# First layer: projections on input times norm weight, with the root applied to the products

## The chip, the cores and the metric

The kernel runs on 1 core of one Trainium2 chip. The metric is the time of one execution on the device in microseconds (us); the whole network is one launch.

## What is computed

Sixteen meta tokens and 1,024 input tokens, each of width 1,024, go through four layers: windowed attention, an mLSTM, an HGRN2 and windowed attention again. Each layer normalizes its input and adds its output to it. The change touches the first layer, an attention layer:

```python
def rmsnorm(x, g):
    xf = x.astype(jnp.float32)
    y = xf * lax.rsqrt(jnp.mean(xf * xf, axis=-1, keepdims=True) + EPS)
    return (y * g.astype(jnp.float32)).astype(x.dtype)

# u = rmsnorm(h, norm_gain[i])
q, k, v, z = _split(u @ w_in, (A_W, A_KVW, A_KVW, A_W))
q = rope(rmsnorm(q.reshape(bsz, lp, A_HEADS, A_HD), q_gain), pos)
k = rope(rmsnorm(k.reshape(bsz, lp, A_KV, A_HD), k_gain), pos)
o = sliding_window_attention(q, k, v, sinks, valid)
return (o * jax.nn.silu(z.astype(jnp.float32))).astype(u.dtype) @ w_out
```

The root `rsqrt(...)` is one number for each token. It is a factor of the whole row of u, and so of q, k, v and z before their own norms and gates.

## The kernel before

The state `x` lies in SBUF with the model width on the partitions: eight tiles of 128 x 1,040 tokens. The tokens go in three chunks of 400, 384 and 256 (`CHUNKS`; chunk 0 has the 16 meta tokens in front). Every matrix is split into a high and a low part of a reduced float format (`split`: ScalarE casts, VectorE subtracts), and each product is three matmuls: high by high, low input by high weight, high input by low weight (`proj`, L228). The split input is `uh` and `ul`, the split weight `wh` and `wl`. Weights come in two raw pieces of 128x512 from two rotating buffers (`wr`, `RAWS`), loaded by SyncE's queue.

TensorE's order is written out by hand as a list of steps with costs: `chain`, `weave` and `later` place a projection's follow-up steps at a delay (`D_K` for keys, `D_Q` for queries) behind its matmuls. The other engines run what the steps issue, in an order that a scheduler sets from priorities and readiness at build time. All engines' queues are in order.

In the head of the first layer, for each chunk, one key tile (two heads) and two query tiles are projected. Before that, `Norm` makes the normalized input: ScalarE squares each tile of x (L352), the squares are added (L356, on VectorE for chunk 0, on GpSimd for chunks 1 and 2), TensorE sums over the partitions with a matrix of ones (L364), ScalarE takes the root by a logarithm and an exponential (L338, L339), and for each of the eight tiles VectorE multiplies x by gain and root (L386) and the result is split into `uh` and `ul`.

A query or key product is then evacuated from PSUM by ScalarE twice, with its gain (L492) and squared (L493); four DMAs on SyncE make a rotated copy (L496); TensorE sums the squares (`stat_q`, L516, tiny products for queries; `stat`, L525, a full one for keys); VectorE applies the rotation (L530 to L534) and splits the result for the scores (`qs`, and the key's rows). Behind the head comes the body: score steps S (L621, L622, then VectorE, an exponential on ScalarE and a product on GpSimd, L635), transposes T (L647) and value products V (L666), woven with the value, query, key and gate projections and the output projections. A gate's evacuation (`gate_proj`) is a sigmoid in five steps and two products on VectorE (L411, L412). The buffers `Sm`, `Ph` and `Pl` of the scores have two copies each, `tmp` tiles (t) six, PSUM eight, and `yh`, a pair of the output projections, three.

Of the kernel before, what the change touches and what calls it, by code (L numbers as in the profile page):

```python
# [15 lines left out]
P = 128  # L16
D = 1024
# [94 lines left out]
def hybrid_kernel(ctx: ExitStack, tc: tile.TileContext, ins, out, layers=(0, 1, 2, 3)):  # L112
# [35 lines left out]
    def psj():  # L148
        return psum("pj", 3)
# [9 lines left out]
    ngain = cpool.tile([P, 4, KT], F32, name="ngain")  # L159
    eps = cpool.tile([P, 1], F32, name="eps")  # L160
    v.memset(eps, EPS)
    one = cpool.tile([P, 1], F32, name="one")
    v.memset(one, 1.0)
# [5 lines left out]

    def load_x(n):  # L170
        c0, cn = CHUNKS[n]
        for k in range(KT):
            sp.dma_start(x[:, k, c0 : c0 + cn], ins["xT"][k, :, c0 : c0 + cn])

    load_x(0)
    sp.dma_start(ngain, ins["ngain"])

# [32 lines left out]

    def proj(src, evac, chunks=CHUNKS):
        st = {}

        def pre():
            st["w"] = weights(src, "m")

        groups = []
        for n, (c0, cn) in enumerate(chunks):
            grp = []
            for part in range(4):  # L220
                def fn(n=n, c0=c0, cn=cn, part=part):
                    if part == 0:
                        st[n] = psj()
                    h, l = st["w"]
                    acc = st[n]
                    for k in (2 * part, 2 * part + 1):
                        for i, (a, b) in enumerate(((h, uh), (h, ul), (l, uh))):
                            pe.matmul(acc[:, :cn], a[:, k, :], b[:, k, c0 : c0 + cn],  # L228
                                      start=(k == 0 and i == 0), stop=(k == KT - 1 and i == 2))
# [111 lines left out]
    class Norm:  # L341
        def __init__(self, i, row=None):
            self.i, self.row, self.acc, self.ps = i, row, {}, {}

        def sq(self, m, n, c0, cn, size=KT):
            if m % size:
                q = tmp()[:, :cn]
            elif self.row is not None and n:
                q = self.row[:, c0 : c0 + cn]
            else:  # L350
                q = (vtile() if n == 2 else tmp())[:, :cn]
            s.activation(q, x[:, m, c0 : c0 + cn], AF.Square)  # L352
            if m % size == 0:
                self.acc[n] = q
            else:
                (v if self.row is None or n == 0 else g).tensor_tensor(self.acc[n], self.acc[n], q, op=ALU.add)  # L356

        def stat(self, n, part=0, parts=1):
            cn = CHUNKS[n][1]

            def fn():
                if part == 0:
                    self.ps[n] = psa()
                pe.matmul(self.ps[n][:, :cn], ones, self.acc[n], start=(part == 0), stop=(part == parts - 1))  # L364
                if part == parts - 1:
                    rstd_from(self.ps[n], self.acc[n], cn, D)

            return [4 * cn * MM, fn, None]

        def squares(self, n, part=0, parts=1):  # L370

            size = KT // parts

            def fn():
                for m in range(part * size, (part + 1) * size):
                    self.sq(m, n, *CHUNKS[n], size)

            return [0.0, fn, None]

# [15 lines left out]
        def units(self, n, t0, t1):  # L395
            return [(t0 + (t1 - t0) * k / KT, self.unit(n, k)) for k in range(KT)]

    def sigmoid_from(z, cn):
        a = tmp()
# [6 lines left out]

    def gate_proj(src, o, chunks=CHUNKS):
        def evac(acc, n, c0, cn):
            cs = slice(c0, c0 + cn)
            a = sigmoid_from(acc[:, :cn], cn)  # L410
            v.tensor_tensor(a[:, :cn], a[:, :cn], acc[:, :cn], op=ALU.mult)  # L411
            v.tensor_tensor(o()[:, cs], o()[:, cs], a[:, :cn], op=ALU.mult)  # L412

        return proj(src, evac, chunks)

    def layer_a(i, j, first, last, fin):
        win, wout = ins["a_win"][j], ins["a_wout"][j]
# [67 lines left out]

        def qk_proj(src, gcol, work, fsplit, ch, t=None):
            late = {}

            def evac(acc, n, c0, cn):
                dst, sq, rot = work(n, c0, cn)  # L490
                late[n] = dst, sq, rot
                s.activation(dst, acc[:, :cn], AF.Identity, scale=R["cons"][:, gcol : gcol + 1])  # L492
                s.activation(sq, acc[:, :cn], AF.Square)  # L493
                for q in range(4):
                    o = q ^ 1
                    sp.dma_start(rot[32 * q : 32 * q + 32], dst[32 * o : 32 * o + 32])  # L496

            def finish(n, c0, cn):
                def factors():
                    b0, bn = CHUNKS[n]  # L500
                    if R.get("cs", (None,))[0] != n:
                        R["cs"] = n, R["mix"].tile([P, 2, 400], F32, tag="cs", name=nm("cs"), bufs=1)
                        sp.dma_start(R["cs"][1][:, :, :bn], ins["rope"][:, :, b0 : b0 + bn].rearrange("a p t -> p a t"))
                    late[n] += (R["cs"][1][:, :, c0 - b0 : c0 - b0 + cn],)

                def stat_q():
# [10 lines left out]
                    z = slice(2 if last and n == 0 else 0, 2 * nb)  # L517
                    s.activation(rq[:, z], st[:, z], AF.Ln, bias=eps, scale=1.0 / 64)
                    s.activation(rq[:, z], rq[:, z], AF.Exp, scale=-0.5)
# [17 lines left out]
                if t is not None:  # L537
                    return [(D_Q[0], [0.0, factors, None]), (D_Q[1], [108 * len(CHUNK_BLOCKS[n]), stat_q, None]),
                            (D_Q[2], [0.0, rope, None]), (D_Q[3], turn)]
                return [(D_K[0], [4 * cn * MM, stat, None]), (D_K[1], [0.0, rope, None]), (D_K[2], turn)]  # L540

            return proj(src, evac, ch), [finish(n, *c) for n, c in enumerate(ch)]

# [20 lines left out]
        def v_proj(src, jj):  # L564
# [7 lines left out]
            def finish(n, c0, cn):  # L572
                def fn():
# [4 lines left out]
                    for k, b in enumerate(CHUNK_BLOCKS[n]):  # L578
# [6 lines left out]
                        src = pt[:nq, P * k : P * k + P].rearrange("p (a c) -> p a c", a=2)  # L585
                        s.copy(parts[:, 0:4:3], src)
                        v.tensor_tensor(parts[:, 1:3], src, parts[:, 0:4:3].bitcast(F32), op=ALU.subtract)

# [105 lines left out]

        zc = {t: gate_proj(win[12 + t], lambda t=t: R["o", t], chunks) for t in range(8)}
# [3 lines left out]
        kg1, kfin1 = qk_proj(win[1], 1, tmps, k_split(1), CHUNKS)  # L699
        vg0, vfin0 = v_proj(win[2], 0)  # L700
        vg1, vfin1 = v_proj(win[3], 1)
        qg = {t: qk_proj(win[4 + t], 0, tmps, q_split(t), chunks, t) for t in range(8)}

# [11 lines left out]
        for n in range(3):  # L715
            parts = [([], ev), tile_of([k0[0][n]], [k0[1][n]]), tile_of([qa[0][n]], [qa[1][n]])]
            if first and n == 0:
                (a, fa), (b, fb) = parts[1:]
                ta = sum(z[0] for z in a)
                parts[1:] = [(a[:2] + b[:2] + a[2:] + b[2:], [(d + ta, z) for d, z in fa + fb])]  # L720
            if first:
                parts += [tile_of([qb[0][n]], [qb[1][n]])]
            elif n == 2:
                parts += [tile_of(*qb)]
            grp, ev = chain(parts)
            head.append(grp)
# [597 lines left out]

    norm = Norm(layers[0], row())

    for k in range(PARTS):
        steps += [norm.squares(0, k, PARTS), norm.stat(0, k, PARTS)]
    steps += [norm.unit(0, k) for k in range(KT)]
    tail = None  # L1330
    for pos, i in enumerate(layers):
# [10 lines left out]
        if i % 3 == 0:  # L1342
            head, body, oa, ob = layer_a(i, i // 3, tail is None, i == 3, fin)
        elif i % 3 == 1:
# [17 lines left out]
        else:  # L1362
            h0, h1 = (sum(z[0] for z in head[k]) for k in range(2))
            seq = flat(head)
            for n, t, h in ((2, h0, h1), (1, 0.0, h0)):
                t0, t1, t2 = (t + z * h for z in FIRST[n - 1])
                later(seq, (t0, norm.squares(n)), (t1, norm.stat(n)), *norm.units(n, t2, t + h))
            head = [seq]
# [5 lines left out]

    ahead, k = 0.0, 0
    while steps[k][2] is None:
        k += 1
    steps[k][2]()
    steps[k][2] = None
    load_x(1)  # L1380
    sp.dma_start(ident, ins["ident"])
    k = 0
    for n, (cost, fn, pre) in enumerate(steps):
# [119 lines left out]
```

## Time and profile before

| | |
|---|---|
| median of 3 runs | 2615.19 us (2614.67 to 2615.76) |
| the profiled execution's own time | 2615.34 us |
| its span | 2613.6 us |
| busy: TensorE, VectorE, ScalarE, GpSimd | 98%, 75%, 65%, 10% |
| first product of the head | 14.08 us |
| first product behind the head | 79.39 us |
| first score step S | 84.66 us |

A row of the timeline gives the start, the length, engine, line, operation, output and inputs, and in brackets the idle time of the engine before it and what ended that. A row of the groups gives a line's instructions: busy us, mean ns of one, and idle time before them. A row of the table by stretch gives the length and each engine's busy time. The busy time of TensorE counts matmuls that overlap and run at half speed, so the pace of products is read from their starts.

### The profile page before, as it was taken

The numbers are of one execution on the slowest core, as the hardware profiler recorded it, in microseconds if no ns is written. First come the engines' busy times: TensorE is split into PE (matmuls) and PEld (weight loads), VectorE is DVE, ScalarE is ACT, GpSimd is POOL, SyncE is SP. The second block draws the span as 40 slices with busy tenths as digits, with TensorE's granted clock in tenths as the row PEclk, the third lists the DMA queues.
The fourth block names the chain that finished last, engine by engine and source line by source line (L and its number), as shares of the span: only waits on it lengthen the run. The fifth ranks groups of instructions, "written<-read, shape, count | busy, mean of one in ns | idle before, by whom it ended". The sixth has DMA issues, their size and how long they took to land.

```text
span 2613.6 us, 54261 instructions
## 1 busy us (share of the span) xinstructions
PE 2565.6 (98%) x20422; PEld 2485.5 (95%) x20422; DVE 1952.1 (75%) x5248; ACT 1689.4 (65%) x4422; POOL 249.1 (10%) x502
## 2 busy tenths in 40 slices
PE   7999999999999999999999999999999999999999
PEld 6999999999999999999999999999999999999999
DVE  6797798785647474646465688988888978887996
ACT  6776767576555555554555757878675857767772
POOL 2221221000000000000000000101000000321330
PEclk8999999999999999999999999999999999999999
DMA  4212111021111111111111111111111113112112
GB/s 130 68 51 85 54 44 48 22 66 58 41 58 41 58 41 51 44 53 41 57 41 50 57 32 37 34 34 34 38 38 31 37 51 92 56 47 84 56 40 79
DMA packets 82582, 135.92 MB, mean 52 GB/s; under 512 B 12032, under 2 KB 35712, under 8 KB 82320
## 3 DMA queue, kind: packets, MB, share of 16 engines
q1 hardware_dynamic: 82320, 132.45, 16.3%
q8 instruction: 161, 2.64, 0.4%
q14 instruction: 101, 0.83, 0.1%
HBM read 117.56 MB, written 4.26 MB: 47 GB/s over the span
## 4 chain that ended last, share of the span: by engine, by line
PE 80%; DVE 9%; ACT 6%; DMA 2%; issue 2%; SPq 1%; POOL 0%; DVEq 0%; ACTq 0%; POOLq 0%
PE pj L228 39%; PE pj L322 16%; PE pj L277 10%; PE po L666 2%; PE pt L647 2%; PE po L909 1%; PE pa L923 1%; PE po L911 1%; PE pm L621 1%; ACT Sm L632 1%; PE pm L622 1%; DVE Sm L629 1%; PE pj L273 1%; PE pm L1161 1%; DMA cs<-in_rope 1%
## 5 line engine op out<-in xcount | busy, mean ns | idle before, releaser
L228 PE MATMUL pj<-uh,wh 128*128 128x256 f32 (+2 forms) x2688 | 915.2, 340 | 9.3 <-ACT uh L194 9.2
L228 PE MATMUL pj<-ul,wh 128*128 128x256 f32 (+2 forms) x2688 | 867.7, 323 | 2.1 <-DVE ul L195 1.9
L228 PE MATMUL pj<-uh,wl 128*128 128x256 f32 (+2 forms) x2688 | 864.6, 322 | 0.0
L228 PEld LDWEIGHTS pj<-uh,wh 128*128 128x128 f32 x2688 | 510.0, 190 | 26.0 <-ACT uh L194 12.5
L228 PEld LDWEIGHTS pj<-ul,wh 128*128 128x128 f32 x2688 | 510.1, 190 | 10.5 <-DVE ul L195 5.4
L228 PEld LDWEIGHTS pj<-uh,wl 128*128 128x128 f32 x2688 | 509.7, 190 | 0.0
L195 DVE TENSOR_TENSOR wl<-wr,wh 128x512 fp32r<-128x512 f32 (+1 forms) x338 | 233.6, 701 | 50.1 <-ACT wh L194 47.1
L194 ACT CAST wh<-wr 128x512 fp32r<-128x512 f32 (+1 forms) x338 | 202.9, 613 | 102.1 <-PE pj L322 32.7
L322 PE MATMUL pj<-yh,wh 128*128 128x384 f32 (+2 forms) x768 | 253.2, 330 | 8.2 <-DVE x L325 6.2
L325 DVE TENSOR_TENSOR x<-x,pj 128x384 f32<-128x384 f32 (+2 forms) x480 | 234.6, 507 | 35.0 <-PE pj L322 33.7
L322 PE MATMUL pj<-yh,wl 128*128 128x384 f32 (+2 forms) x768 | 245.5, 320 | 0.0
L322 PE MATMUL pj<-yl,wh 128*128 128x384 f32 (+2 forms) x768 | 245.5, 320 | 0.0
L277 PE MATMUL pj<-wh,uh 128*128 128x256 f32 (+1 forms) x768 | 232.2, 302 | 0.0
L277 PE MATMUL pj<-wl,uh 128*128 128x256 f32 (+1 forms) x768 | 216.5, 282 | 0.0
L277 PE MATMUL pj<-wh,ul 128*128 128x256 f32 (+1 forms) x768 | 216.2, 282 | 0.0
L635 POOL TENSOR_TENSOR Sm<-Sm,s 128x512 f32<-128x512 f32 (+2 forms) x136 | 142.2, 1046 | 450.6 <-DVE s L634 435.8
L632 ACT ACTIVATE Sm<-Sm,s 128x257 f32<-128x257 f32 (+2 forms) x272 | 130.8, 482 | 78.9 <-DVE s L629 74.7
L404 ACT ACTIVATE t<-t 128x384 f32<-128x384 f32 (+2 forms) x240 | 117.9, 491 | 82.9 <-DVE t L403 80.8
L403 DVE SCALAR_TENSOR_TENSOR t<-pj,t 128x384 f32<-128x384 f32 (+2 forms) x192 | 98.7, 514 | 80.1 <-ACT t L402 78.4
L322 PEld LDWEIGHTS pj<-yh,wh 128*128 128x128 f32 x768 | 144.5, 188 | 11.9 <-DVE x L325 7.3
L194 ACT CAST yh<-r 128x384 fp32r<-128x384 f32 (+2 forms) x120 | 57.1, 478 | 152.0 <-PE pj L322 139.9
L277 PEld LDWEIGHTS pj<-wh,uh 128*128 128x128 f32 x768 | 144.6, 188 | 2.2
(255 smaller groups left out, 5434.0 us busy)
## 6 DMA issues: line engine op xcount, KB each, us to landing
wr<-in_b_win SPq DMA_DIRECT2D x124, 256.0 KB, 2.9
wr<-in_a_win SPq DMA_DIRECT2D x80, 256.0 KB, 2.9
wr<-in_c_win SPq DMA_DIRECT2D x64, 256.0 KB, 2.7
wr<-in_a_wout SPq DMA_DIRECT2D x32, 256.0 KB, 2.8
wr<-in_b_wout SPq DMA_DIRECT2D x32, 256.0 KB, 2.8
t<-t SPq DMA_DIRECT2D x104, 48.0 KB, 1.9
cs<-in_rope SPq DMA_DIRECT2D x11, 400.0 KB, 3.4
cs<-in_rope SPq DMA_DIRECT2D x11, 384.0 KB, 3.4
```

Of the source, the lines that this page charges most:

```text
L194: s.copy(h, src)
L195: v.tensor_tensor(l, src, h.bitcast(F32), op=ALU.subtract)
L228: pe.matmul(acc[:, :cn], a[:, k, :], b[:, k, c0 : c0 + cn], start=(k == 0 and i == 0), stop=(k == KT - 1 and i == 2))
L277: pe.matmul(acc[:cn, :nc], a[:, k, c0 : c0 + cn], m[:, kk, :], start=(k == 0 and j == 0), stop=(k == KT - 1 and j == 2))
L322: pe.matmul(acc[:, :cn], a[:, k, mc], b, start=(k == 0 and i == 0), stop=(k == 1 and i == 2))
L325: v.tensor_tensor(x[:, m, c0 : c0 + cn], x[:, m, c0 : c0 + cn], acc[:, :cn], op=ALU.add)
L403: v.scalar_tensor_tensor(a[:, :cn], z, 0.0, a[:, :cn], op0=ALU.min, op1=ALU.subtract)
L404: s.activation(a[:, :cn], a[:, :cn], AF.Exp)
L632: s.activation(Sm[:nq, u, : nk + 1], Sm[:nq, u, : nk + 1], AF.Exp, scale=-1.0, bias=st[:nq, u : u + 1], accum_out=den[:nq, u : u + 1])
L635: g.tensor_tensor(Sm[:nq, :, :nk], Sm[:nq, :, :nk], den[:nq].rearrange("p (u c) -> p u c", c=1).to_broadcast([nq, 2, nk]), op=ALU.mult)
L647: pe.transpose(pt[:kn, ki, u, :nq], Sm[:nq, u, ko : ko + kn], ident[:nq, :nq])
L666: pe.matmul(po[:, :, q0 - g0 : q0 - g0 + nq], V[pair // 2, kb][:kn, P * hh : P * hh + P], w[part][:kn, ki, :, :nq], start=(ki == 0 and par ...
```

## The change

`Norm` serves the later layers alone. For the first layer a class `Scale` takes its place. It splits x times the gain, without the root (`unit`), so the products need nothing but x and the weights. Squares of x are made and added on GpSimd for chunks 0 and 2, and on ScalarE with adds on VectorE for chunk 1; they are written to the three `yh` buffers. `sums` makes the root later, as a row over the tokens and as columns for blocks of tokens, and stores the row in memory; `fetch` reads it back into all partitions. The root then comes behind the products: the key's evacuation and each gate's multiply by it on VectorE, the values' split takes it as a scale, and the query statistic adds a term with EPS in place of it, since the query's own norm removes it.

The head's order becomes query, query, key; the key's evacuation in the head is put off (`held`, `D_EVAC`), the chains behind it get longer delays, and query 1 writes into the scores' buffers `Ph`, `Pl` and `Sm` (`idle`). The loads go weights first, half of x, weights, the other half.

```diff
-PARTS = 4
-FIRST = (0.2, 0.8, 0.85), (0.2, 0.75, 0.8)
+FIRST = (0.3, 0.2, 0.9), (0.0, 1.1, 1.9)
+D_K0, D_K1 = (5000.0, 7000.0, 9000.0), (5000.0, 7000.0, 9000.0)
+D_Q0 = 5500.0, 8000.0, 7000.0, 9000.0
+D_EVAC = 3000.0
+SUMS = 1.22, 1.95, 2.95
...
+    class Scale:
...
+            def fn():
+                gain = ngain[:, self.i, k : k + 1]
+                s.activation(uh[:, k, cs], x[:, k, cs], AF.Identity, scale=gain)
+                v.scalar_tensor_tensor(ul[:, k, cs], x[:, k, cs], gain, uh[:, k, cs].bitcast(F32),
+                                       op0=ALU.mult, op1=ALU.subtract)
...
+                for m in range(KT):
+                    q = tpool.tile([P, 400], F32, tag="yh", name=nm("sq"), bufs=YS)[:, :cn] if m else acc
+                    z = x[:, m, c0 : c0 + cn]
+                    if n == 1:
+                        s.activation(q, z, AF.Square)
+                    else:
+                        g.tensor_tensor(q, z, z, op=ALU.mult)
+                    if m:
+                        (v if n == 1 else g).tensor_tensor(acc, acc, q, op=ALU.add)
...
+                for k, b in enumerate(bs):
+                    q0 = blk(b)[0] - c0
+                    pe.matmul(pc[:, k : k + 1], acc[:, q0 : q0 + P], ones[:, 0:1], start=True, stop=True)
+                r, e = (z[:, bs[0] : bs[-1] + 1] for z in (self.rcol, self.ecol))
+                s.activation(e, pc[:, : len(bs)], AF.Identity, bias=self.eps2, scale=EPS / D)
+                s.activation(r, pc[:, : len(bs)], AF.Ln, bias=eps, scale=1.0 / D)
+                s.activation(r, r, AF.Exp, scale=-0.5)
+                pr = psa()
+                pe.matmul(pr[:, :cn], ones, acc, start=True, stop=True)
+                rstd_from(pr, acc, cn, D)
+                sp.dma_start(self.dram[c0 : c0 + cn], acc[0:1])
...
+        def fetch(self, dst, c0, cn):
+            sp.dma_start(dst[:, :cn], self.dram[c0 : c0 + cn].partition_broadcast(P))
...
         def evac(acc, n, c0, cn):
             cs = slice(c0, c0 + cn)
-            a = sigmoid_from(acc[:, :cn], cn)
-            v.tensor_tensor(a[:, :cn], a[:, :cn], acc[:, :cn], op=ALU.mult)
+            z = acc[:, :cn]
+            if scale is not None:
+                z = rs[n][:, :cn]
+                v.tensor_tensor(z, z, acc[:, :cn], op=ALU.mult)
+            a = sigmoid_from(z, cn)
+            v.tensor_tensor(a[:, :cn], a[:, :cn], z, op=ALU.mult)
...
+        def idle(n, c0, cn):
+            z = [R["mix"].tile([P, 2, 2, P], F32, tag=z, name=nm(z), bufs=2) for z in ("Ph", "Pl")]
+            z = [y.rearrange("p a u q -> p (a u q)") for y in z]
+            z.append(R["mix"].tile([P, 2, 257], F32, tag="Sm", name=nm("Sm"), bufs=2).rearrange("p u k -> p (u k)"))
...
+                if first and t is None:
+                    v.tensor_tensor(sq, sq if fetched else scale.row[:, c0 : c0 + cn], z, op=ALU.mult)
+                    z = sq
...
+                        v.scalar_tensor_tensor(rq.rearrange("p (k c) -> p k c", c=2),
+                                               st[:, z].rearrange("p (k c) -> p k c", c=2), 1.0 / 64, e,
+                                               op0=ALU.mult, op1=ALU.add)
```

At the program's start, TensorE before sums squares (`pa`) ahead of the first product (`pj`):

```order
L364 MATMUL pa_148<-t_143,ones 128x400
L364 MATMUL pa_148<-t_150,ones 128x400
L364 MATMUL pa_148<-t_156,ones 128x400
L364 MATMUL pa_148<-t_162,ones 128x400
L228 MATMUL pj_211<-uh,wh_96 128x400
```

and now begins with the products:

```order
L232 MATMUL pj_214<-uh,wh_90 128x400 [waits Activation_49]
L232 MATMUL pj_214<-ul,wh_90 128x400 [waits DVE_49]
L232 MATMUL pj_214<-uh,wl_91 128x400
L232 MATMUL pj_214<-uh,wh_90 128x400 [waits Activation_49]
L232 MATMUL pj_214<-ul,wh_90 128x400 [waits DVE_49]
```

The sums moved behind; the first products wait for ScalarE's and VectorE's split of x alone.

On ScalarE in the head, before, the squares of chunk 1 (`t` from x) end ahead of the first key's and query's evacuations (`pj`):

```order
L352 ACTIVATE t_241<-x 128x384
L352 ACTIVATE t_244<-x 128x384
L352 ACTIVATE t_247<-x 128x384
L352 ACTIVATE t_250<-x 128x384
L492 ACTIVATE r_271<-pj_211,cons_207 128x400
L493 ACTIVATE r_272<-pj_211 128x400
L492 ACTIVATE t_292<-pj_224,cons_207 128x400
L493 ACTIVATE t_293<-pj_224 128x400
```

and now, behind the last split of x, whose high part is `uh` (`sq`: squares of chunk 1 in the `yh` buffers; `pj_214` and `pj_227`: the two queries' products of chunk 0):

```order
L401 ACTIVATE uh<-x,ngain 128x256 [waits DMAHW7_49]
L419 ACTIVATE sq_245<-x 128x384 [waits Pool_49]
L419 ACTIVATE sq_248<-x 128x384 [waits Pool_49]
L419 ACTIVATE sq_251<-x 128x384 [waits Pool_49]
L419 ACTIVATE sq_254<-x 128x384 [waits DVE_49]
L576 ACTIVATE t_280<-pj_214,cons_188 128x400 [waits DMAHW1_49,DVE_49,PE_49]
L419 ACTIVATE sq_257<-x 128x384 [waits DVE_49]
L419 ACTIVATE sq_260<-x 128x384 [waits DVE_49]
L419 ACTIVATE sq_263<-x 128x384 [waits DVE_49]
L577 ACTIVATE t_281<-pj_214 128x400
L576 ACTIVATE Ph_305<-pj_227,cons_188 128x400 [waits PE_49]
L577 ACTIVATE Pl_306<-pj_227 128x400
```

The squares of chunk 1 stand behind all splits and now wait for GpSimd, and the queries' evacuations stand behind the squares.

What they wait for is the end of GpSimd's queue in the head, the last squares of chunk 2 and their adds, which now has 30 operations ahead of the first copy for the scores (`Sm`):

```order
L421 TENSOR_TENSOR sq_205<-x 128x256 [waits DMAHW5_49]
L423 TENSOR_TENSOR r_86<-r_86,sq_205 128x256 [waits Pool_49]
L421 TENSOR_TENSOR sq_208<-x 128x256 [waits DMAHW6_49]
L423 TENSOR_TENSOR r_86<-r_86,sq_208 128x256 [waits Pool_49]
L421 TENSOR_TENSOR sq_211<-x 128x256 [waits DMAHW7_49]
L423 TENSOR_TENSOR r_86<-r_86,sq_211 128x256 [waits Pool_49]
```

where there were the adds alone, with the squares on ScalarE:

```order
L356 TENSOR_TENSOR r_95<-r_95,t_439 128x256
L356 TENSOR_TENSOR r_95<-r_95,t_442 128x256
L356 TENSOR_TENSOR r_95<-r_95,t_445 128x256
L356 TENSOR_TENSOR r_95<-r_95,t_448 128x256
L635 TENSOR_TENSOR Sm_804<-Sm_804,s_806 16x2x16
```

GpSimd's queue grew from 14 adds (of chunks 1 and 2) to 16 squares and 14 adds (of chunks 0 and 2).

More of the change, by code (lines that the diff above doesn't have):

```diff
@@ L223, in fn @@
                         st[n] = psj()
+                    if part == 1 and early is not None:
+                        early(n, c0, cn)
                     h, l = st["w"]
@@ L693, in mixers @@
             return segs
-        zc = {t: gate_proj(win[12 + t], lambda t=t: R["o", t], chunks) for t in range(8)}
+        zc = {t: gate_proj(win[12 + t], lambda t=t: R["o", t], chunks, scale) for t in range(8)}
         oc = {t: proj_out(wout[t - 1], wout[t], lambda k, t=t: R["o", t - 1 + k], chunks,
@@ L698, in layer_a @@
         kg0, kfin0 = qk_proj(win[0], 1, work_rows(3), k_split(0), CHUNKS)
-        kg1, kfin1 = qk_proj(win[1], 1, tmps, k_split(1), CHUNKS)
+        kg1, kfin1 = qk_proj(win[1], 1, tmps, k_split(1), CHUNKS, fetched=first)
         vg0, vfin0 = v_proj(win[2], 0)
         vg1, vfin1 = v_proj(win[3], 1)
-        qg = {t: qk_proj(win[4 + t], 0, tmps, q_split(t), chunks, t) for t in range(8)}
+        qg = {t: qk_proj(win[4 + t], 0, idle if first and t == 1 else tmps, q_split(t), chunks, t) for t in range(8)}
         def q_pair(p):
@@ L1323, in ahead_of_end @@
         steps[k:k] = first
[L1325 to L1329, printed above, removed]
+    norm = Scale(layers[0])
+    steps += [norm.unit(0, k) for k in range(KT)] + [norm.squares(0)]
     tail = None
@@ L1373, in hybrid_kernel @@
     steps += seq
[L1375 to L1379, printed above, removed]
+    pres = [z for z in steps if z[2] is not None]
+    for z, k0, k1 in ((pres[0], 0, 4), (pres[1], 4, 8)):
+        z[2]()
+        z[2] = None
+        load_x(0, k0, k1)
+    pres[2][2]()
+    pres[2][2] = None
     load_x(1)
     sp.dma_start(ident, ins["ident"])
-    k = 0
+    ahead, k = 0.0, 0
     for n, (cost, fn, pre) in enumerate(steps):
```

158 lines of the change are left out of this document (102 added, 56 removed).

## The prediction

> **What bounds the kernel now.** I read the page's totals, then busy time by stretch, then the timeline of the first 85 us, then the waits of TensorE.
>
> ```profile
> span 2613.6 us, 54261 instructions
> PE 2565.6 (98%) x20422; PEld 2485.5 (95%) x20422; DVE 1952.1 (75%) x5248; ACT 1689.4 (65%) x4422; POOL 249.1 (10%) x502
> ```
>
> TensorE is busy 98% of the span, so the end moves only by what TensorE waits or runs slowly. The timed execution took 2615.34 us, 1.7 us more than its span, and lies 0.15 us from the median of the runs, 2615.19; I carry the sum on 2615.34. The change touches the first layer alone, so I look for lost time there: length, then busy us and count of PE, PEld, DVE, ACT and POOL, then the granted clock, the DMA share and GB/s.
>
> ```profile
> 0.00:10.00 10.00, 4.28 (x6) 1.91 (x7) 2.73 (x8) 6.30 (x11) 0.52 (x5) 1.00 0.80 260
> 10.00:20.00 10.00, 6.89 (x18) 5.19 (x17) 8.29 (x16) 6.56 (x14) 0.17 (x1) 0.71 0.73 257
> 40.00:60.00 20.00, 16.32 (x75) 15.02 (x75) 13.92 (x27) 13.32 (x32) 5.80 (x7) 0.83 0.18 50
> 60.00:80.00 20.00, 17.20 (x84) 14.98 (x84) 13.23 (x30) 12.53 (x32) 0.00 (x0) 0.66 0.14 36
> 160.00:320.00 160.00, 159.58 (x1093) 155.66 (x1092) 130.22 (x333) 113.21 (x317) 34.91 (x54) 1.00 0.20 60
> 320.00:420.00 100.00, 96.22 (x685) 91.93 (x684) 90.71 (x258) 73.06 (x217) 30.92 (x49) 1.00 0.13 40
> 440.00:490.00 50.00, 48.86 (x308) 48.00 (x308) 44.18 (x95) 22.66 (x50) 0.89 (x11) 1.00 0.06 15
> ```
>
> The loss sits before 80 us: empty time, then half-speed stretches. From 160 to 320 us TensorE has 0.4 us of idle time; from 320 to 420 it has 3.8 us, while VectorE is at 90.7%.
>
> ```profile
> 14.08 0.66 PE L228 MATMUL pj<-uh,wh 128*128 128x400 f32 x1 [2.75 <-ACT uh L194]
> 34.87 0.39 PE L228 MATMUL pj<-uh,wh 128*128 128x384 f32 x1
> 44.83 0.68 PE L228 MATMUL pj<-uh,wh 128*128 128x384 f32 x1 [2.90 <-ACT uh L194]
> 51.75 0.34 PE L228 MATMUL pj<-uh,wh 128*128 128x384 f32 x1
> 79.39 0.35 PE L228 MATMUL pj<-uh,wh 128*128 128x400 f32 x1
> 84.66 0.17 PE L621 MATMUL pm<-r,qs 128*16 128x16 f32 x1
> ```
>
> The first product starts at 14.08, the second chunk at 34.87, the first product behind the head at 79.39, the first score step (S) at 84.66. The row at 44.83 follows an idle 2.90 us; products then run at half speed until 51.75, about 7 us.
>
> **Part by part. The start.** The root goes from the path: x is issued at 0.74, and ScalarE starts on it at 3.62.
>
> ```profile
> 0.74 3.71 SPq L173 DMA_DIRECT2D x<-in_xT  x8
> 3.62 1.02 ACT L352 ACTIVATE t<-x 128x400 f32<-128x400 f32 x2 [1.61 <-DMA x<-in_xT]
> ```
>
> Now the gains and two weight pieces (0.5 MB) go first, three issues of 0.46 us. At 260 GB/s, the first stretch's rate, they hold x up by about 2 us: x at about 5.8, first product near 6.4, 7.7 us earlier. The second tile's weight pieces wait on SyncE until the first tile's splits free the two raw buffers, near 6.3, and the second half of x queues behind them; it lands by about 12, still ahead of the splits that need it, so I cost that at nothing.
>
> **GpSimd's queue, the term that decides.** GpSimd gets 15 operations of 128x400 and 15 of 128x256. Its rows, and those of VectorE beside them:
>
> ```profile
> L356 POOL TENSOR_TENSOR r<-r,t 128x384 f32<-128x384 f32 x7 | 7.5, 1068 | 22.3 <-ACT t L352 21.9
> L356 POOL TENSOR_TENSOR r<-r,t 128x256 f32<-128x256 f32 x7 | 5.8, 828 | 17.5 <-ACT t L352 17.0
> 19.83 1.35 POOL L356 TENSOR_TENSOR r<-r,t 128x384 f32<-128x384 f32 x1 [18.78 <-ACT t L352]
> 20.23 1.93 DVE L386 SCALAR_TENSOR_TENSOR t<-x,ngain,t 128x400 f32<-128x400 f32 x2
> 28.92 2.06 POOL L356 TENSOR_TENSOR r<-r,t 128x384 f32<-128x384 f32 x2
> 205.56 2.11 DVE L195 TENSOR_TENSOR wl<-wr,wh 128x512 fp32r<-128x512 f32 x2
> L195 DVE TENSOR_TENSOR wl<-wr,wh 128x512 fp32r<-128x512 f32 x9 | 5.9, 688 | 1.4 <-ACT wh L194 1.4
> 205.72 1.40 POOL L635 TENSOR_TENSOR Sm<-Sm,s 128x512 f32<-128x512 f32 x1 [3.00 <-DVE s L634]
> L195 DVE TENSOR_TENSOR ul<-t,uh 128x400 fp32r<-128x400 f32 x8 | 4.3, 569 | 0.0
> L195 DVE TENSOR_TENSOR ul<-t,uh 128x256 fp32r<-128x256 f32 x8 | 3.3, 423 | 0.7 <-ACT uh L194 0.5
> 12.83 1.73 DVE L386 SCALAR_TENSOR_TENSOR t<-x,ngain,t 128x400 f32<-128x400 f32 x3 [1.71 <-ACT t L339]
> ```
>
> Two adds on an idle VectorE take 2.06 us; beside VectorE one takes 1.35, and two scaled products, 0.58 us each in the row at 12.83, take 1.93 there. At 205.6 two splits, elsewhere 0.69 us each, take 2.11 around one GpSimd operation, which itself takes 1.40. So the two engines take turns, operation by operation, and each pays most of the other's length. Low bound of the queue, as if alone: 15x1.07+15x0.83 = 28.5 us. Taking turns with VectorE's splits: 15x1.34+15x0.96 = 34.5 us, which is 1.03 us alone (half of the row at 28.92) and some 0.3 for a split of 0.57, and about 0.73 and 0.23 for chunk 2's, whose splits take 0.42. I take the second, since VectorE has some 30 splits and 7 adds of that kind queued in just this time: the rows at 205 are the nearest, a VectorE queue that is never empty. From x at 5.8, GpSimd ends at 40.3 (low: 34.4). Its copies for the scores stand behind the thirty, and are not wanted before S.
>
> ScalarE's squares of chunk 1 take the three buffers that GpSimd's squares of chunk 2 give back, so the first three wait for GpSimd's 11th, 13th and 15th operation on that chunk, and everything behind them on ScalarE's queue waits too, the evacuations of both first queries among it.
>
> ```profile
> L352 ACT ACTIVATE t<-x 128x384 f32<-128x384 f32 x7 | 3.1, 512 | 0.0
> L492 ACT ACTIVATE t<-pj,cons 128x400 f32<-128x400 f32 x2 | 1.2, 588 | 0.0
> L493 ACT ACTIVATE t<-pj 128x400 f32<-128x400 f32 x2 | 1.0, 499 | 0.0
> ```
>
> From GpSimd's end: five squares, two evacuations, two squares of sums: 5x0.51+2x0.59+2x0.50 = 4.7 us. TensorE's small products for the query statistics come free at 45.0 (low: 39.1). TensorE arrives there at about 33. In chunk 0 a split comes free every 1.34 us instead of every 0.57; the twelve splits that two query tiles and the key's first weights wait for put the end of its 72 products at about 26.5 instead of 34.87. Then 30 products of chunk 1 (30x0.176 = 5.3) and the first sums (about 1) follow. So it idles some 12 us, and the lead of 8 is spent.
>
> **From there to the first S:** 42 products of 128x384, 72 of 128x256, 24 of 128x400. The first two rows are of the chain of waits (start, us, what):
>
> ```profile
> 53.60 2.11 PE pj L228 x12
> 132.50 0.70 PE pj L228 x6
> L525 PE MATMUL pa<-r,masks 128*128 128x384 f32 x2 | 0.8, 486 | 0.0
> L516 PE MATMUL pa<-masks,t 128*128 128x2 f32 x36 | 5.6, 273 | 0.0
> ```
>
> That is 42x0.176+72x0.117+24x0.18 = 20.1, and about 5 for statistics and sums. Two waits come on top. The first key's statistic needs 12 operations of ScalarE (root columns, root, chunk 1's first query, query roots, the key) at some 0.4 us, 4.9 in all, while TensorE has 2.3 us of work: 2.6. The second key's statistic needs the second sums, their root and 14 operations of ScalarE that stand ahead of it, some 9.5 us, against 46 products and small ones, 5.9 us: 3.6. Each stop is followed by about 6 us at half speed, as at 44.83, so 2x3. Sum 20.1+5+2.6+3.6+6 = 37.3: first S at 82.3 instead of 84.66, gain 2.3 us. Bounds: 39.1+25.1 = 64 (nothing waits behind the restart, gain 20) and 90 (each wait doubled, with its half speed; loss 5).
>
> The page "TensorE: Matmul & The Clock Gate", Part 1, of the Trainium skill states that a busy window of about 3.4 us sustained releases the clock. This trace had about 7 us after 44.83; by the page each of my stops would have 3.4 slow us instead of 6 and cost 1.3 less, 2.6 us in all, a time of 2618.
>
> **Buffers of the scores.** Query 1's rotated copy sits in one of the two score buffers until its chunk 2 is done, so the first three S steps share one and each waits for the transposes of the one before: about 1.4 us (0 to 4), from a reciprocal, an exponential and a GpSimd product of about 1 us each time. The wider delays of the head's chains add no instruction. The root's store to memory waits on SyncE for its exponential, and behind it wait the rotations of chunk 1 and of the key; these land before VectorE reaches them in the count above, so I add nothing, and 2 us if they don't.
>
> **The body.** Each of 24 gate evacuations gets one VectorE product with the fetched root, two operations now read SBUF twice and take turns with GpSimd, 18 query statistics get a small VectorE operation (as the reciprocal below) and key tile 1 three products.
>
> ```profile
> L411 DVE TENSOR_TENSOR t<-t,pj x24: 406/552/573, 152.7 to 444.7; 128x400 f32<-128x400 f32 x8, 128x384 f32<-128x384 f32 x8, 128x256 f32<-128x256 f32 x8
> 205.48 0.17 DVE L634 RECIPROCAL s<-s 128x2 f32<-128x2 f32 x1
> PE pj L322 <- DVE x L325: 1.1, 1, 1.1
> ```
>
> 24x0.52+18x0.17+3x0.52 = 17 us, plus turns: 36 operations, GpSimd busy 31% (30.92 of 100), half a us each: 5. VectorE's 22 us more fall on 330 us. From 160 to 320 it has 30 us free: I take 1. From 320 to 420 about 6 fall on 9.3 free us, where TensorE already loses 3.8: I take 3. From 440 to 490 about 4 fall on 5.8, and TensorE already waited 1.1 there for VectorE: 2. The 27 fetches behind which SyncE's weight loads queue, and roots held early in the six shared buffers: 0.5 (0 to 6). Body 6.5; ends 0 (all covered) and 28 (nothing covered). No gain here: nothing is removed.
>
> Sum: 2615.34-2.3+1.4+6.5 = 2620.9, so **2621 us**.
>
> **Rivals.** (A) *The queue runs as if alone*: GpSimd ends at 34.4, S at 82.3-5.9 = 76.4, gain 8.3; the body loses 3: 2610. For: the adds at 28.92 keep 1.03. Against: the rows at 20.23 and 205.56. (B) *Faster*: besides, TensorE restarts at 39 without further stops, S near 70, gain 14.5, body 3: 2604. For: chunks 1 and 2 are split long before. Against: ScalarE's queue between the sums. It decides if less than 3 us of waits remain behind the restart. (C) *The body's VectorE saturates*: from 320 to 490 nearly all of its added 10 us pass to TensorE and the fetches hold weight loads up: 2631. For: 90.7% and 88% busy. Against: 30 us free before 320.
>
> **How the numbers follow.** Forecast 0.42 (2614 to 2627), A 0.24 (2606 to 2613), B 0.16, C 0.18. 0.2%, 5.2 us, is about what a measurement of this kernel tells from no change. Slower by more than that (over 2620.4): 0.42x0.62+0.18 = 0.44, with rounding 0.45. Faster (under 2610.0): half of A and B, 0.28, taken as 0.30. Same: 0.25. The range 2604 to 2632 leaves out half of B and a third of C.
>
> **What would show it.** Right: first product near 6.4; GpSimd's second fifteen ending near 40; VectorE's splits at 1.0 to 1.4 us until then; TensorE idle some 12 us before the query statistics, half clock behind; first S at 80 to 84; more idle time from 320 to 490 than the 4.9 us of now. Wrong: GpSimd's end before 36, S before 76, or TensorE's idle time in the body unchanged.

## The result, and the profile after

The changed kernel takes 2629.34 us (median of 5 runs, 2625.68 to 2631.48) against 2615.19 of before: 14 us more. The ratio is 1.0049, with a 95% interval of 1.0034 to 1.0064. Its profiled span is 2627.9 us, 14.3 more than the span of before, so this trace can be read against that of before directly.

The totals of the page after:

```profile
span 2627.9 us, 54397 instructions
PE 2567.7 (98%) x20434; PEld 2491.8 (95%) x20434; DVE 1974.3 (75%) x5282; ACT 1688.6 (64%) x4415; POOL 270.7 (10%) x518
```

TensorE is busy for 2 us more and the span is 14 longer: the other 12 are idle time. Rows of the table by stretch after (columns as before):

```profile
10.00:20.00 10.00, 8.16 (x34) 5.99 (x35) 10.00 (x9) 5.81 (x12) 10.00 (x9) 1.00 0.74 232
160.00:320.00 160.00, 153.35 (x1020) 148.34 (x1018) 129.93 (x336) 109.49 (x301) 32.32 (x49) 0.98 0.25 71
320.00:420.00 100.00, 95.17 (x672) 91.88 (x671) 90.64 (x251) 68.78 (x203) 32.44 (x48) 0.98 0.18 52
420.00:440.00 20.00, 18.14 (x111) 17.85 (x110) 17.37 (x41) 14.86 (x38) 3.77 (x4) 0.91 0.30 90
440.00:490.00 50.00, 50.00 (x314) 49.71 (x313) 44.01 (x94) 26.61 (x56) 0.42 (x1) 1.00 0.13 39
```

From 10 to 20 us VectorE and GpSimd are both busy 10.00 of 10.00 us, and VectorE runs 9 operations in that time, where before it ran 16 in 8.29 us. From 160 to 320 us TensorE has 6.65 us of idle time, where it had 0.4, and VectorE is *not* busier there than before (129.93 against 130.22). From 320 to 490 us the idle time grows from 4.9 to 6.7 us, all of it before 440.

The head after, TensorE's timeline:

```profile
6.76 0.70 PE L232 MATMUL pj<-uh,wh 128*128 128x400 f32 x1 [6.76 <-ACT uh L401]
...
25.78 0.34 PE L232 MATMUL pj<-uh,wh 128*128 128x384 f32 x1
...
40.95 1.87 PE L600 MATMUL pa<-masks,t 128*128 128x2 f32 x8 [8.17 <-ACT t L577]
...
48.93 0.33 PE L232 MATMUL pj<-uh,wh 128*128 128x384 f32 x1
...
65.75 1.49 PE L617 MATMUL pa<-r,masks 128*128 128x384 f32 x2 [2.48 <-ACT r L577]
...
76.64 0.17 PE L724 MATMUL pm<-r,qs 128*16 128x16 f32 x1
```

and GpSimd's, the first square of chunk 0, the first of chunk 2 and the last add:

```profile
6.06 0.85 POOL L421 TENSOR_TENSOR r<-x 128x400 f32<-128x400 f32 x1 [5.02 <-DMA x<-in_xT]
24.71 0.94 POOL L421 TENSOR_TENSOR r<-x 128x256 f32<-128x256 f32 x1
36.91 0.92 POOL L423 TENSOR_TENSOR r<-r,sq 128x256 f32<-128x256 f32 x1
```

VectorE's splits of chunks 1 and 2, and the small product on the gains (L491) that ScalarE's first evacuation reads:

```profile
21.32 15.04 DVE L402 SCALAR_TENSOR_TENSOR ul<-x,ngain,uh 128x384 fp32r<-128x384 f32 x16
37.23 0.62 DVE L491 TENSOR_SCALAR cons<-cons 128x16 f32<-128x16 f32 x1
```

GpSimd's last add ends at 37.83 and VectorE's small product at 37.85: two chains end at the same time.

The first S comes at 76.64 instead of 84.66: the head *gains* 8.0 us. The first product of layer B comes at 500.44 instead of 489.08. So from the first S to there the body loses 19.4 us. What TensorE waited for between 85 and 500 us (us in total, times, longest):

```profile
PE pa L617 <- ACT t L577: 5.2, 2, 2.7
PE pm L724 <- DVE Pl L753: 4.0, 2, 2.5
PE pt L750 <- POOL Sm L738: 2.8, 3, 1.9
```

The first row is new. L617 is the statistic of key tile 1. The timeline around it, rows of SyncE, VectorE and TensorE in order of time:

```profile
244.53 2.41 SPq L580 DMA_DIRECT2D t<-t  x4
247.04 1.15 SPq L449 DMA_DIRECT2D t<-scaled  x1
252.13 0.56 DVE L574 TENSOR_TENSOR t<-t,pj 128x384 f32<-128x384 f32 x1 [4.59 <-DMA t<-scaled]
253.94 1.65 PE L617 MATMUL pa<-t,masks 128*128 128x384 f32 x2 [2.52 <-ACT t L577]
255.87 0.53 SPq L449 DMA_DIRECT2D t<-scaled  x1
260.27 0.42 DVE L574 TENSOR_TENSOR t<-t,pj 128x256 f32<-128x256 f32 x1 [3.00 <-DMA t<-scaled]
262.28 0.48 PE L617 MATMUL pa<-t,masks 128*128 128x256 f32 x1 [2.73 <-ACT t L577]
```

It reads as a chain. The fetch of the root for one chunk (L449) stands on SyncE behind the four rotations of the chunk before (L580). Those wait for that chunk's evacuation, which waits for that chunk's own fetch. The fetch is issued at 247.04; VectorE, idle for 4.59 us, multiplies at 252.13; ScalarE squares; TensorE's statistic starts at 253.94. The next fetch goes out at 255.87 and its statistic starts at 262.28, 8.3 us after the other.

### The profile page after: what moved, and what is told of

The parts are those of the page before. It is cut to its first block, busy times and chain, and to the rows that moved or that the text cites. A ratio compares the mean times of both kernels' runs of the same rounds, so it can differ in the third digit from the quotient of the medians.

```text
span 2627.9 us, 54397 instructions
## 1 busy us (share of the span) xinstructions
PE 2567.7 (98%) x20434; PEld 2491.8 (95%) x20434; DVE 1974.3 (75%) x5282; ACT 1688.6 (64%) x4415; POOL 270.7 (10%) x518
## 4 chain that ended last, share of the span: by engine, by line
PE 79%; DVE 9%; ACT 6%; DMA 2%; issue 2%; POOL 2%; SPq 0%; DVEq 0%; ACTq 0%; POOLq 0%
PE pj L232 38%; PE pj L326 16%; PE pj L281 10%; PE po L769 2%; PE pt L750 1%; PE po L1011 1%; PE pa L1025 1%; PE po L1013 1%; DVE Sm L732 1%; ACT Sm L735 1%; DVE wl L197 1%; PE pm L1263 1%; PE pj L277 1%; PE pm L724 1%; PE pm L725 1%
## 5 line engine op out<-in xcount | busy, mean ns | idle before, releaser
L326 PE MATMUL pj<-yh,wh 128*128 128x384 f32 (+2 forms) x768 | 254.1, 331 | 8.3 <-DVE x L329 6.4
L326 PE MATMUL pj<-yh,wl 128*128 128x384 f32 (+2 forms) x768 | 246.6, 321 | 0.0
L326 PE MATMUL pj<-yl,wh 128*128 128x384 f32 (+2 forms) x768 | 246.6, 321 | 0.0
L326 PEld LDWEIGHTS pj<-yh,wh 128*128 128x128 f32 x768 | 145.0, 189 | 12.5 <-DVE x L329 7.9
L281 PEld LDWEIGHTS pj<-wl,uh 128*128 128x128 f32 x768 | 145.1, 189 | 1.9
```

Source lines behind the costliest of these rows:

```text
L281: pe.matmul(acc[:cn, :nc], a[:, k, c0 : c0 + cn], m[:, kk, :], start=(k == 0 and j == 0), stop=(k == KT - 1 and j == 2))
L326: pe.matmul(acc[:, :cn], a[:, k, mc], b, start=(k == 0 and i == 0), stop=(k == 1 and i == 2))
```

## The experiments

Eleven kernels were timed against the kernel before, 5 rounds each. The table gives the ratio to before with its interval, and from each trace the start of the first query statistic, of the first S, of the first output product (L326, L322 before) and of the first product of layer B. The ratio of the changed kernel is from its own comparison; a difference of 0.0010 in ratio is 2.6 us. The intervals reach 2.4 to 3.9 us to each side, so a difference between two rows tells little below about 5 us. The other columns are of one execution each, and that of `k1_ahead` was 4.5 us faster than its median. Behind the start of layer B the trace of before takes 2124.5 us and those of the twelve others, which share their code there, 2124.3 to 2127.5.

| kernel | ratio | query stat. | first S | first output | layer B |
|---|---|---|---|---|---|
| before | 1 | 32.87 | 84.66 | 172.58 | 489.08 |
| changed | 1.0049 (1.0034 to 1.0064) | 40.95 | 76.64 | 168.19 | 500.44 |
| k1_noroot | 1.0019 (1.0010 to 1.0028) | 40.54 | 75.69 | 168.56 | 492.75 |
| k1_ahead | 1.0030 (1.0019 to 1.0040) | 41.27 | 77.26 | 168.81 | 494.80 |
| gate_noroot | 1.0028 (1.0016 to 1.0039) | 41.07 | 76.70 | 168.28 | 496.02 |
| gate_nofetch | 1.0040 (1.0027 to 1.0052) | 41.04 | 76.91 | 168.45 | 499.52 |
| own_squares | 1.0032 (1.0019 to 1.0044) | 41.44 | 74.25 | 165.77 | 498.47 |
| no_gpsimd | 1.0008 (0.9999 to 1.0017) | 28.82 | 61.59 | 157.90 | 493.11 |
| dummy_gp | 1.0039 (1.0027 to 1.0052) | 41.28 | 75.83 | 167.10 | 501.44 |
| no_idle | 1.0047 (1.0033 to 1.0061) | 40.97 | 77.34 | 167.40 | 498.15 |
| keys_noroot | 0.9998 (0.9989 to 1.0007) | 40.72 | 71.65 | 162.58 | 489.18 |
| keys_noroot_nogp | 0.9943 (0.9930 to 0.9957) | 28.61 | 60.35 | 151.03 | 475.36 |
| keys_nogp_noidle | 0.9937 (0.9924 to 0.9949) | 29.02 | 58.86 | 151.00 | 472.69 |

**The fetches of key tile 1.** First, key tile 1 without the root (`held` is true for key tile 0 alone; key tile 1 is evacuated straight from PSUM, without a fetch):

```diff
-                if first and t is None:
+                if held:
                     v.tensor_tensor(sq, sq if fetched else scale.row[:, c0 : c0 + cn], z, op=ALU.mult)
```

> Key tile 1 of the first layer is evacuated straight from PSUM, without the root's fetch and product (its own norm takes the root out again, up to EPS). Theory F (the fetches of key 1 stand on SyncE behind the rotations of the chunk before and make a chain of some 9 us a chunk): the idle times of 2.52, 2.73 and 0.95 us before key 1's statistics at 254 to 264 us go, and the slow stretches behind them; 2629.3 - 8.6 = 2620.7 us (2619 to 2623). Theory V (VectorE's added work sets the body's loss): three products of 0.5 us less, 2628 us.

Measured: 0.30% less than the changed kernel, 7.8 us by the ratios and 7.7 at layer B's start (492.75), as theory F has it. Of the waits there one is left, from TensorE's waits between 236 and 268 us:

```profile
PE pt L676 <- ACT t L669: 0.8, 1, 0.8
```

Then the product kept, and the three fetches issued together:

```diff
             def early(n, c0, cn):
-                late[n] = work(n, c0, cn)
-                scale.fetch(late[n][1], c0, cn)
+                if n == 0:
+                    for m, (d0, dn) in enumerate(ch):
+                        late[m] = [None, tmp()[:, :dn], None]
+                        scale.fetch(late[m][1], d0, dn)
+                late[n][0], late[n][2] = tmp()[:, :cn], tmp()[:, :cn]
```

> Key tile 1 keeps its root product; its three fetches are issued together at its first chunk, into three of the six shared buffers, ahead of the rotations. Theory F: the products no longer wait for a landing, most of the 8.6 us goes, 2622 us (2620.5 to 2625; the three buffers held longer may give a microsecond or two back). Theory V: no change, 2629.

Measured: 0.19% less, 5.0 us, about as much as the intervals can tell; F expected 4 to 9. The key's statistics wait no more, but the values' evacuation (L670) now comes late (TensorE's waits):

```profile
PE pt L677 <- ACT t L670: 4.2, 1, 4.2
```

So the place of the fetches in SyncE's queue was the wait, not the three products. Fetching ahead pays part of it back at the values' evacuation. That evacuation writes one of the six shared buffers, three of which are now taken at once for roots; that this is why it comes late is not shown.

**The gates.** First the fetch and the product left out together (`gate_proj` without `scale`), then the fetch alone, with a tile of x in place of the root. Both kernels leave the root out of the gates, so their output is not the layer's; they serve to find the cost. The edit of the second:

```diff
-            scale.fetch(rs[n], c0, cn)
...
-                v.tensor_tensor(z, z, acc[:, :cn], op=ALU.mult)
+                v.tensor_tensor(z, x[:, 0, cs], acc[:, :cn], op=ALU.mult)
```

> The first layer's gates are made without the root (left out: the root's fetch and VectorE's product in each of 24 gate evacuations). Theory F: what the gates cost is the loss at 340 to 450 us, 6 us more than before the change; 2629.3 - 5.5 = 2624 us (2622 to 2626). Theory V: 24 products of 0.52 us and their turns are most of the 19 us the body lost: 2629.3 - 12 = 2617 us.

> Each gate's product on VectorE stays, but reads a resident tile of x in place of the fetched root (the root is left out of the gates; no fetch is issued for them). Without both, fetch and product, the time fell by 5.5 us against the changed kernel. Theory P (it was VectorE's products): 2629.3 - 1 = 2628 us. Theory D (it was the 24 fetches, in front of SyncE's weight loads and rotations): 2624 to 2625 us.

Without both the time fell by 0.21%, 5.5 us, near theory F's 5.5 and not V's 12, though the intervals leave room for 1 to 10. TensorE's waits from 320 to 450 us, first after, then in gate_noroot:

```profile
PE pm L724 <- DVE Pl L753: 4.0, 2, 2.5
PE pt L750 <- POOL Sm L738: 2.0, 2, 1.9
```

```profile
PE pm L724 <- DVE Pl L753: 3.7, 2, 2.0
PE pt L750 <- POOL Sm L738: 1.2, 3, 0.5
```

These waits are shorter by only 1.1 us, so they are not the whole of it. Without the fetch alone it is 0.09%, 2.4 us, inside the intervals of both. At layer B's start it is 0.9 us, against 4.4 without both. So the traces, one execution each, speak for the products and the time does not contradict it; the 24 fetches are not shown to cost anything. `gate_noroot` also leaves free the shared buffer that each root held, and no run separates that from the product.

**The head: who waits for GpSimd.** Squares of chunk 1 in buffers that GpSimd does not use:

```diff
-  q = tpool.tile([P, 400], F32, tag="yh", name=nm("sq"), bufs=YS)[:, :cn] if m else acc
+  q = acc if m == 0 else tmp()[:, :cn] if n == 1 else tpool.tile([P, 400], F32, tag="yh", ...)[:, :cn]
```

> ScalarE's squares of chunk 1 go into the shared tmp buffers, so they no longer wait for GpSimd. Theory Q (the query statistics wait for GpSimd's end through these buffers): TensorE's idle 8.2 us before the first query statistics falls to under 3, the slow stretch behind it shortens, first S at about 69 instead of 76.6, 2629.3 - 7 = 2622 us (2621 to 2624). Rival W (the wait moves to what stands behind, the first sums' root or key 0's product): first S at 74 to 75, 2627 us.

Measured: 0.17% less, 4.4 us, which the intervals alone do not tell from nothing. Theory Q fell: the first S came at 74.25, as the rival had it, though what is late next was neither of the two that the rival named. It is VectorE's queue. Rows of its timeline, ScalarE's and TensorE's in this kernel:

```profile
31.73 0.69 PE L232 MATMUL pj<-ul,wh 128*128 128x384 f32 x1 [2.11 <-DVE ul L402]
32.48 6.34 DVE L402 SCALAR_TENSOR_TENSOR ul<-x,ngain,uh 128x384 fp32r<-128x384 f32 x7
39.06 0.60 ACT L576 ACTIVATE t<-pj,cons 128x400 f32<-128x400 f32 x1 [8.07 <-DVE cons L491]
```

Seven splits take 0.91 us each beside GpSimd. TensorE waits for them, and ScalarE's first evacuation waits 8.07 us for the small product on the gains (L491) that is queued behind them. (Here some of VectorE's adds also stand ahead of these splits.) So all squares were taken from GpSimd:

```diff
-                    if n == 1:
+                    if n < 3:
                         s.activation(q, z, AF.Square)
...
-                        (v if n == 1 else g).tensor_tensor(acc, acc, q, op=ALU.add)
+                        v.tensor_tensor(acc, acc, q, op=ALU.add)
```

> All squares of x in the head on ScalarE, all adds on VectorE; GpSimd has nothing in the head. Theory L (VectorE and GpSimd take turns: VectorE's splits of 0.57 us take 0.9 to 1.4 beside GpSimd): VectorE's first 40 us hold 16.5 us of splits and 10.8 of adds instead of 37 us of splits in turns, ScalarE's some 28 us of splits and squares; both end near 34, TensorE restarts at 36 instead of 40.95; 2629.3 - 5 = 2624 us (2622 to 2626). Rival W (the sheer work of ScalarE and VectorE, 14 adds and 16 squares more, takes the place of the turns): restart at 40 to 42, 2629 us or more.

Measured: 0.41% less, 10.7 us, twice what theory L gave. ScalarE and VectorE do 30 operations more, and yet TensorE's first query statistic starts at 28.82 without a wait (its timeline; the second row is the first V, which waits 4.33 us instead of 1.13):

```profile
28.82 0.95 PE L600 MATMUL pa<-masks,t 128*128 128x2 f32 x8
...
73.65 0.39 PE L769 MATMUL po<-Ph,v 16*128 16x32 f32 x1 [4.33 <-DVE v L687]
```

The first S comes 15.1 us earlier than in the changed kernel, the first product of layer B only 7.3: half of a lead won in the head is lost again behind it.

Does GpSimd hurt by being late, or by running? The next kernel adds to this one GpSimd work that nobody reads:

```diff
+                    if n != 1:
+                        for _ in range(2 if m else 1):
+                            w = tpool.tile([P, 400], F32R, tag="yl", name=nm("idle"), bufs=YS)[:, :cn]
+                            g.tensor_tensor(w.bitcast(F32), z, z, op=ALU.mult)
```

> As with no squares on GpSimd in the head (2617.9 us, splits of x 573 ns each on VectorE), but GpSimd now multiplies tiles of x into buffers that nothing reads: 15 operations of 128x400 and 15 of 128x256, which no engine waits for. Theory L (VectorE and GpSimd take turns, whoever waits): VectorE's 24 splits take about 1.0 us again instead of 0.57 and its 21 adds nearly 1, TensorE restarts at 42 or later instead of 28.8, the time goes back to 2628 us or above. Rival B (the changed kernel lost only by waiting for GpSimd's results through buffers): splits stay at 0.57, 2618 us.

Measured: ratio 1.0039 instead of 1.0008, 8.1 us more. The first query statistic is back at 41.28 and the first S at 75.83, within a microsecond of the changed kernel:

```profile
41.28 0.37 PE L604 MATMUL pa<-masks,t 128*128 128x2 f32 x1 [4.17 <-ACT t L581]
```

VectorE's groups of the first 45 us (busy us, mean ns), in the changed kernel, in no_gpsimd, and in dummy_gp with GpSimd's own group:

```profile
L402 DVE SCALAR_TENSOR_TENSOR ul<-x,ngain,uh 128x400 fp32r<-128x400 f32 (+2 forms) x24 | 24.3, 1081 | 0.5 <-ACT uh L401 0.5
L197 DVE TENSOR_TENSOR wl<-wr,wh 128x512 fp32r<-128x512 f32 x6 | 7.0, 1186 | 3.8 <-ACT wh L196 3.8
```

```profile
L402 DVE SCALAR_TENSOR_TENSOR ul<-x,ngain,uh 128x400 fp32r<-128x400 f32 (+2 forms) x24 | 12.9, 573 | 0.7 <-ACT uh L401 0.6
L423 DVE TENSOR_TENSOR r<-r,sq 128x400 f32<-128x400 f32 (+2 forms) x21 | 10.7, 515 | 1.2 <-ACT uh L401 0.5
L197 DVE TENSOR_TENSOR wl<-wr,wh 128x512 fp32r<-128x512 f32 x6 | 4.1, 689 | 4.3 <-ACT wh L196 4.1
```

```profile
L402 DVE SCALAR_TENSOR_TENSOR ul<-x,ngain,uh 128x400 fp32r<-128x400 f32 (+2 forms) x20 | 17.8, 928 | 0.2 <-ACT uh L401 0.2
L423 DVE TENSOR_TENSOR r<-r,sq 128x400 f32<-128x400 f32 (+2 forms) x21 | 15.2, 729 | 1.2 <-ACT sq L419 0.5
L197 DVE TENSOR_TENSOR wl<-wr,wh 128x512 fp32r<-128x512 f32 x6 | 7.0, 1192 | 3.8 <-ACT wh L196 3.8
L427 POOL TENSOR_TENSOR idle<-x 128x400 f32<-128x400 f32 (+1 forms) x30 | 30.5, 1052 | 5.0 <-DMA x<-in_xT 5.0
```

A split of x costs VectorE 573 ns on average alone and 928 to 1,081 in the two kernels with GpSimd work, a split of weights 689 and 1,190. These means mix shapes; of 128x400 alone a split takes 630 ns in no_gpsimd, 1,117 in dummy_gp and 1,220 in the changed kernel. In dummy_gp GpSimd ends at 36.5 us, and the four splits of 128x256 behind that take 479 ns each, as in no_gpsimd (481). GpSimd's results are read by nobody in dummy_gp, so it is the running, not the result. The Trainium skill, page "SBUF — State Buffer", section "Who interferes with whom", states that a VectorE instruction with two inputs in SBUF contends with a GpSimd instruction that reads SBUF, and the one that issues second blocks until the other has finished. These traces agree that the two lengthen each other's operations: the split of 128x400 grew by 0.49 us from no_gpsimd to dummy_gp. That is less than half of a GpSimd operation of 128x400 there (1.18 us), so that each waits for the other's whole length is not what they show.

**The score buffers.**

```diff
-  qg = {t: qk_proj(win[4 + t], 0, idle if first and t == 1 else tmps, q_split(t), chunks, t) for t in range(8)}
+  qg = {t: qk_proj(win[4 + t], 0, tmps, q_split(t), chunks, t) for t in range(8)}
```

> Query 1 of the head works in the six shared buffers as other queries do, not in the score buffers Ph, Pl and Sm. By the prediction's term the first score steps share one buffer and lose 1.4 us (0 to 4): the idle 0.40 and 0.94 us before the second and third transposes go, 2629.3 - 1.4 = 2628 us. Rival: the six shared buffers are too few in the head and a query waits for one, 2631 us or more.

Measured: 1.0047 against 1.0049: nothing that can be told, and the 1.4 us in question is below what these intervals tell. The short waits before the transposes go, but the head's second key statistic waits 2.7 us instead of 2.5 and the first V 2.0 instead of 1.1.

**Both causes taken out.** Since a key's own norm takes the root out again up to EPS, neither key needs it. Key 0 is then evacuated at once (`held = False`), key 1 without a fetch.

> Neither key tile gets the root (its own norm takes it out again, up to EPS), so key 0's evacuation in the head is not put off and waits for no root. Theory F with key 0: key 1's 7.8 us as measured, and the idle 2.48 us before key 0's second statistic with its slow stretch, 4 us: 2629.3 - 12 = 2617.5 us. Rival W (key 0 waited for ScalarE's queue, not for the root): 2621.5 us, as without key 1's root alone.

> Both: no root on the keys, and nothing on GpSimd in the head. If the two gains are apart: 2629.3 - 12 - 5 = 2612.5 us, a little under the kernel before the change; if the head's wait only moves to ScalarE's squares: 2617.5 us.

> No root on the keys, nothing on GpSimd in the head (2601.7 us), and query 1 in the shared buffers as well. By the prediction's term for the score buffers: 2600 us; if the shared buffers run short: 2604 us or more.

keys_noroot is 0.51% under the changed kernel, 13.3 us, where 12 was expected: level with before. With GpSimd idle in the head it is 0.9943, 15 us faster than before and 28 faster than the changed kernel. The two gains together are 24 (13.3 + 10.7); the 4 more are within the intervals, though the first V waits 0.4 us here and 4.33 in no_gpsimd. Query 1 in the shared buffers makes 0.9937, not to be told from 0.9943.

## Why the prediction was right and wrong

The kernel is slower, as forecast, and the time lies in the range, but 8 us above the forecast and above the forecast's own bounds of 2614 to 2627. The two large terms were both wrong, and partly cancel: the first S came 5.7 us earlier than forecast, and from there to layer B the kernel lost 19.4 us where 7.9 (1.4 and 6.5) were forecast. With the head as forecast and the rest as measured the sum would be 2635, outside the range: that the time lies inside is partly luck.

- **The start**, as forecast: first product at 6.76 (6.4), chunk 1 at 25.78 (26.5 for the end of chunk 0), and TensorE's stop begins at 32.8 (33).
- **GpSimd's queue in turns**, right in kind, a little too long: it ends at 37.83 (40.3). Its first fifteen took 18.65 us, 1.24 each instead of 1.34, the others 0.87 instead of 0.96.
- **What stands behind it**: the statistics come at 40.95 (45.0), 3.1 us behind GpSimd and not 4.7; TensorE idles 8.17 us (12). That ScalarE waits through the three `yh` buffers is what the trace shows, but the prediction took this for the only late chain. VectorE's queue is a second one of the same length: its splits of chunks 1 and 2, slowed by the same turns, run from 21.32 to 36.36, and L491 behind them ends at 37.85. own_squares takes the first chain away and the statistics still come at 41.44. The words "chunks 1 and 2 are split long before" in rival B are not so.
- **From there to the first S**: 35.7 us (37.3). The first key's statistic had no wait (2.6 expected), the second 2.48 (3.6). The gain at S is 8.0 instead of 2.3, the size of rival A's 8.3, but not by rival A alone, which had GpSimd end at 34.4: of the 5.7 us more, GpSimd's earlier end gave 2.5, the shorter way from there to the statistics 1.6 and the way to S another 1.6. The prediction's upper bound for S, 90, does not follow from its terms: with both waits and their half speed doubled they give 94.5.
- **The score buffers**, 1.4: idle times of 0.40 and 0.94 us are in the trace, but the time of no_idle tells nothing of that size. In its trace the stretch from the first S to the first output takes 90.1 us instead of 91.6 (87.9 before), while the first S comes 0.7 later. The term is neither shown nor refuted.
- **The body**: 6.5 was forecast, 19.4 came. The products on VectorE were sized about rightly: about 6 forecast, 5.5 without the gates' root (fetch, product and buffer together, with a wide interval). Their place was not: 2 us were put between 440 and 490, where TensorE has no idle time. The step that failed is "The 27 fetches behind which SyncE's weight loads queue", priced at 0.5 (0 to 6) together with the buffers: three of them, key tile 1's, cost 7.8 us with their products by k1_noroot, and 5.0 of it went by moving the fetches alone. The prediction looked at what the fetches hold up behind them on SyncE and not at what stands ahead of them and waits: the rotations, which depend on the fetch before.
- **Rival C** gave about the measured time, but not by its mechanism: from 320 to 420 us VectorE was no busier than before (90.64 against 90.71), TensorE's idle time from 320 to 490 grew by 1.8 us and not by nearly 10, and the largest loss lies before 320, where VectorE stood idle while the chain ran.

Open: at layer B's start the two body terms are 7.7 and 4.4 us, which leaves about 7 of the 19.4. Of these, 3.6 fall between the first S and the first output (the lead shrinks from 8.0 to 4.4), before any key 1 and with few gates, and no run here isolates them. Part of it may be no cost of the body at all: no_gpsimd shows that a lead in the head shrinks behind it. Behind layer B's start the changed kernel takes 2.9 us more than before (2127.5 against 2124.5). That is within the scatter of single traces there: k1_ahead and keys_noroot, with the changed kernel's code, take 2124.3 and 2124.5.

## What to carry to other kernels

Before work is moved to GpSimd because it is idle, look at what VectorE does at that time: here VectorE's operations with two operands in SBUF took up to twice as long beside it, even where nobody waited for GpSimd, and the kernel was 10.7 us faster with the same work on ScalarE and VectorE. A transfer that a computation needs should not be issued, on an in-order queue, behind transfers that depend on that same computation one step earlier: follow such a chain once round before pricing it as "small". And where a factor is removed again by a later norm (here up to EPS), leave it out rather than fetch it.

## What the runs showed of the hardware

That work which nothing reads can cost 8 us was unexpected in its size: 30 GpSimd operations with a total of 30.5 us lengthened VectorE's splits and adds of the first 45 us by about 12 us together (40.0 us in dummy_gp with four splits left to come, 27.7 in no_gpsimd). And the clock came back at different times after a stop: after 40.95 products run at half speed until 48.93, 8.0 us, of which the first 3.4 us are 16 products of 128x2; after 253.94, with full products at once, it took some 3 us, as these rows of the changed kernel show (0.33 us from start to start, then 0.17):

```profile
256.39 0.54 PE L232 MATMUL pj<-uh,wh 128*128 128x400 f32 x1
256.72 0.52 PE L232 MATMUL pj<-ul,wh 128*128 128x400 f32 x1
...
257.27 0.34 PE L232 MATMUL pj<-uh,wh 128*128 128x384 f32 x1
257.44 0.34 PE L232 MATMUL pj<-ul,wh 128*128 128x384 f32 x1
```

The Trainium skill, page "TensorE: Matmul & The Clock Gate", Part 1, states about 3.4 us of sustained work. The second stop agrees (some 3 us). The first, 8.0 us, agrees roughly if the small products are not counted as work: 4.6 us then remain, from 44.38 to 48.93. No run here settles whether they count.
